# Masked first-token products, a deeper queue of raw weights and later bias reads in a two-layer hybrid attention block

## The chip, the cores and the metric

One core of a Trainium2 chip runs the whole program. The time is device microseconds of one execution, as the median of several. The engines are PE (TensorE, matmuls), DVE (VectorE), ACT (ScalarE), POOL (GpSimd) and SP (SyncE, which here only issues weight loads). Each works through its own instructions strictly in order and waits on semaphores for the others.

## What is computed

A sequence of 272 tokens (16 learned "meta" tokens, then 256 inputs) of width 1024 goes through two layers. Each layer has three kinds of attention on slices of one projection (A: eight heads that attend to the 64 keys an indexer scores highest; B: four differential heads; C: four retention heads), an output projection, and a feed-forward part with a squared ReLU. All is float32.

```python
h = concat([meta, x])                          # 272 x 1024
for l in range(2):
    u = rmsnorm(h, norm_mix[l])
    qa, ka, va, qi, ki, wi, qb, kb, vb, qc, kc, vc, gc = split(u @ w_in[l])
    a_out = sparse_indexer_attention(qa, ka, va, qi, ki, wi, bias_a, 64)
    b_out = rmsnorm(diff_attention(qb, kb, vb, bias_b, lam)) * (1 - lambda_init)
    ret = retention(rotary(qc), rotary(kc), vc)
    c_out = silu(gc) * rmsnorm(ret)
    h = h + concat([a_out, b_out, c_out]) @ w_out[l]
    h = h + square(relu(rmsnorm(h, norm_ff[l]) @ w_ff1[l])) @ w_ff2[l]
out = rmsnorm(h, final_norm)[16:]
```

Tokens are laid along the free axis in most tiles (128 features on the partitions, 272 tokens in a row). The first 16 tokens are handled apart from the two blocks of 128 tokens: their keys and values stand as small block-diagonal tiles, one block of 16 columns for each head that shares the 128 partitions, so that one matmul serves two or four heads.

## The kernel before

The weights are cut into 206 tiles of 128x1024 ("units"): in each layer 31 of the input projection, 8 of the output projection, 64 of the feed-forward part. A matmul in float32r loses low bits, so each unit is taken as two parts. ACT rounds the raw tile to `hi` (line 167), DVE or POOL makes `lo = raw - hi` (line 179; POOL for the units listed in `POOL_LO`), and PE runs three matmuls for each of eight slices, `hi` times the high part of the input, `hi` times its low part, `lo` times its high part (lines 186 to 188, 24 matmuls for a unit).

The program is one list written out by hand. The function `slot` (line 187 on) emits unit i: matmuls, and between them, at six places called evac, none, quarter, half, most and all, whatever was registered for this slot and place. In the middle of slot i stand `to_hi(i+3)`, `to_lo(i+2)` and `load(i+5)`. The table `PLACES` gives for each step of the attention numbers p; p // 6 is the slot in the layer, p % 6 the place in it. So "70" is slot 11, place "most". `AFTER` does the same relative to the unit whose product a step evacuates. What an engine does is thus in the order of these numbers, engine by engine, and a step that waits holds up what stands behind it on its engine.

Raw tiles come through `load` (line 147): one DMA of 512 KB on SP's queue into one of three buffers (`bufs=3`), so the load of unit i+5 waits until `lo` of unit i+2 has been made. The bias goes another way: `bias_write` puts a table into DRAM in 32 shifted copies (line 378, tile `scr`), and four calls of `bias_read` (line 383) fetch it, 32 partitions each and all 12 heads at once, into `nb`; `late_constants` (lines 345, 346) fetches rotary tables and decays. These are issued by ACT, on a queue of their own.

Steps that the change touches:

- `e_ki` (429, 430): the indexer's key is scaled into `kf`, then copied to `kh` by DVE.
- `e_v` (475 to 478): DVE scales a value unit out of PSUM into `vt` and copies two blocks of 64x16 into `vbdT`.
- `e_kbd` (507, 508): two DVE copies of 64x16 from the rotated key `kr`, which POOL has summed, into `kbdT`, four times two copies in all.
- `meta_softmax` (574 on), in the first layer alone, for the B heads (`b_soft`) and the A heads (`a_soft`): step one copies blocks from `kb` or `ka` into `kmB` or `kmA` on DVE (577, eight copies each); step two is two or four small matmuls, a bias, a minimum, a subtraction (592) and an exponential on ACT (593); step three sums and divides (601).
- `a_keys` (649) and `b_keys` (720): DVE copies the columns of the first tokens into `pm` and `wm`, 16 and 8 times.
- `b_pair`, `b_norm`, `b_keys`, `b_keys2`: scores of two B heads on PE, softmax on DVE and ACT, scaling on POOL (709), combination on DVE (714), transposes on PE.
- `a_bias` (617, 618), `a_pair`, `a_norm`, `a_keys`: the same for A heads, with mask plus bias on POOL.

Of the kernel before, what the change touches and what calls it, by code (L numbers as in the profile page):

```python
# [28 lines left out]
C_ID, C_ONES, C_COS, C_SIN, C_NEG, C_DEC, C_DECM, C_EXP = 0, 128, 256, 528, 800, 1072, 2608, 2880  # L29
C_ALL = 2896  # L30
P_MIX, P_FF, P_DN, P_RN = 0, 16, 32, 34
# [23 lines left out]
    "rot_tables": (99,),  # L55
    "e_kbd": (146, 157),
    "c_pair": (158, 163),
# [3 lines left out]
    "b_first": (91,),  # L61
    "b_soft": (76, 84, 86),
    "a_soft": (124, 130, 136),
    "a_pv": (175, 181, 187, 195),
    "factor": (11, 12, 17),
}

# [30 lines left out]
def block_kernel(ctx: ExitStack, tc: tile.TileContext, W, hin, cst, onehot, rbe, par, fin, dlam, out):  # L98
# [48 lines left out]
    def load(i, parts=1):  # L147
        if i >= DEPTH * N_UNITS or i in raws:
            return
        raw = wpool.tile([128, 8, 128], F, name="raw", bufs=3)  # L150
        n = 8 // parts
        for a in range(parts):
            nc.sync.dma_start(raw[:, a * n:a * n + n], W[i // N_UNITS, i % N_UNITS][:, a * n:a * n + n])
        raws[i] = raw
# [35 lines left out]
    def slot(i, ps, cols, xs, first=True, last=True, ks=tuple(range(8)), then=None):  # L190
        fire(i, "evac")
        fire(i, "none")
        if ps is None:
            ps = acc_bank()
        wt = split.pop(("hi", i)), split.pop(("lo", i))
        mm(ps[:, cols], wt, xs, ks[:2], first, False)
        fire(i, "quarter")
        mm(ps[:, cols], wt, xs, ks[2:4], False, False)
        if then is None:
            if i % N_UNITS != N_IN + 1:  # L200
                to_hi(i + 3)
# [12 lines left out]
        return ps, wt  # L214
# [13 lines left out]
    for _ in range(10):  # L228
        PE.matmul(idle[:, :128], z, z, start=True, stop=True)
    raws[0] = wpool.tile([128, 8, 128], F, name="raw", bufs=3)  # L230
    for a in range(0, 8, 2):
# [108 lines left out]
    to_hi(2)  # L340
    load(3)
    load(4)

    def late_constants():
        nc.scalar.dma_start(cs[:, C_COS:C_NEG], cst[:, C_COS:C_NEG])
        nc.scalar.dma_start(cs[:, C_DEC:C_EXP], cst[:, C_DEC:C_EXP])
# [33 lines left out]

    def bias_read(a):
        s = bcast["scr"]
        nc.scalar.dma_start(nb[32 * a:32 * a + 32],
                          bass.AP(tensor=s.tensor, offset=s.offset + 127 - 32 * a, ap=[[4799, 32], [400, 12], [1, T]]))

# [26 lines left out]
    def mixer(l):  # L412
# [6 lines left out]
        factor_to_rows(b, key, 0, False)  # L419

        def e_ki(ps):
            bc = bcast[key]
            f = ta("kf")
            k2 = ck([128, 2, T], R, "ki")
            kh, kl = k2[:, 0], k2[:, 1]
            V.tensor_tensor(f[64:128], ps[64:128, :T], bc[64:128], OP.mult)
            V.tensor_copy(kh[64:128], f[64:128])  # L430
# [27 lines left out]
        def e_mul(ps, name, m, n, n0, scale=None):  # L458
            bc = bcast[key]
            if name not in st:  # L460
                st[name] = ck([128, n, T], F, name)
            o = st[name][:, m, n0:]
            if scale is None:
                V.tensor_tensor(o, ps[:, n0:T], bc[:, n0:], OP.mult)  # L464
            else:
                V.scalar_tensor_tensor(o, ps[:, n0:T], scale, bc[:, n0:], OP.mult, OP.mult)

        def b_split(ps, name, m, n0, scale):
            if name not in st:
# [26 lines left out]
        def e_rot(ps, name, m, n0):  # L496
# [68 lines left out]

        def meta_softmax(name, plan, q, k, km, bias):

            tiles = km.shape[1]
            per = 8 // tiles
            rows = 128 // per  # L570
            x = {}

            def one():
                for i in range(tiles):
                    for a in range(per):
                        r = slice(rows * a, rows * a + rows)
                        V.tensor_copy(km[r, i, 16 * a:16 * a + 16], st[k][r, i, 0:16])  # L577

            def two():
# [23 lines left out]

            for p, f in zip(PLACES[plan], (one, two, three)):
                place(b, p, f)
# [105 lines left out]
        def b_keys(hd):  # L711
# [147 lines left out]

# [47 lines left out]
        def finish():  # L907
# [19 lines left out]
    def ffn_rows():  # L927
# [52 lines left out]
        def second(i, k):  # L980
# [138 lines left out]
def _constants(np):  # L1119
# [12 lines left out]
    for hd in range(4):  # L1132
# [78 lines left out]
```

## Time and profile before

| | us |
|---|---|
| median of 3 runs (740.35 to 743.11) | 741.5 |
| the profiled execution, device time | 742.43 |
| its span, first to last instruction | 740.6 |
| PE busy | 710.3 |
| DVE, ACT, POOL busy | 495.2, 374.5, 163.8 |

The span falls into the start (0 to 20 us), the first layer's attention ("first mixer", 20 to 146), output projection and feed-forward with the second layer's first units (146 to 403), the second layer's attention ("second mixer", 403 to 508), its output projection and feed-forward (508 to 730) and the last normalisation (730 to 741). Matmuls are pipelined, so a PE that is shown busy may still run at half its clock; the granted clock (PEclk) tells that.

### The profile page before, as it was taken

What the parts mean: (1) busy time and instruction counts of PE and PEld (TensorE: products, weight loads), DVE (VectorE), ACT (ScalarE), POOL (GpSimd) and SP (SyncE); (2) the same over time, 40 slices, a digit from 0 to 9 for tenths busy, and PEclk for the clock granted to TensorE, in tenths of its full rate; (3) what the DMA queues carried; (4) which work ended last, traced back from release to release, by engine and by line L of the source; (5) the groups of instructions that cost most, each with busy time, mean ns of one, the idle gap of its engine ahead of it and who ended that gap; (6) DMA issues with size and microseconds to landing.
All of it is one profiled execution on the core that took longest, in us unless ns stands there. A gap on an engine that the chain in (4) does not pass through costs nothing.

```text
span 740.6 us, 13376 instructions
## 1 busy us (share of the span) xinstructions
PE 710.3 (96%) x5248; PEld 666.3 (90%) x5248; DVE 495.2 (67%) x970; ACT 374.5 (51%) x695; POOL 163.8 (22%) x139
## 2 busy tenths in 40 slices
PE   8998899899999999999999998989999999999996
PEld 7987788789999999999999987978899998998995
DVE  6679869865877666464646897697486555555554
ACT  6425555435556555343435556553376445545543
POOL 3537544213200000000004758340140000000000
PEclk9999999899999999999999999998999999999998
DMA  7586323224545555646453533332356555555551
GB/s 233 140 223 219 97 105 108 77 76 141 191 155 195 171 171 172 190 156 195 156 187 114 176 121 117 108 107 86 114 170 221 178 186 196 188 177 206 186 171 57
DMA packets 34403, 115.53 MB, mean 156 GB/s; under 512 B 3971, under 2 KB 6308, under 8 KB 34340
## 3 DMA queue, kind: packets, MB, share of 16 engines
q1 hardware_dynamic: 31824, 111.00, 45.2%
q10 hardware_dynamic: 2516, 3.68, 2.4%
q8 instruction: 41, 0.67, 0.4%
q14 instruction: 22, 0.18, 0.1%
HBM read 113.00 MB, written 1.66 MB: 155 GB/s over the span
## 4 chain that ended last, share of the span: by engine, by line
PE 75%; DVE 15%; issue 3%; POOL 3%; DMA 3%; ACT 1%; SPq 0%; POOLq 0%; ACTq 0%; DVEq 0%
PE mm L186 19%; PE mm L188 19%; PE mm L187 18%; PE att L977 11%; DMA raw<-w 2%; DVE lo L179 2%; DVE acc L546 1%; DVE ry L503 1%; DVE m L544 1%; DVE wm L720 1%; POOL lo L179 1%; PE att L780 1%; DMA h<-hin 1%; DVE bp L555 1%; DVE kmB L577 1%
## 5 line engine op out<-in xcount | busy, mean ns | idle before, releaser
L167 ACT ACTIVATE hi<-raw 128x1024 fp32r<-128x1024 f32 x204 | 214.7, 1056 | 186.9 <-PE mm L187 133.0
L186 PE MATMUL mm<-uh,hi 128*128 128x272 f32 (+1 forms) x1008 | 298.6, 296 | 2.5 <-DVE ka L464 2.0
L188 PE MATMUL mm<-uh,lo 128*128 128x272 f32 (+1 forms) x1008 | 292.2, 290 | 3.5 <-POOL lo L179 2.7
L187 PE MATMUL mm<-ul,hi 128*128 128x272 f32 (+1 forms) x1008 | 291.1, 289 | 0.4
L179 DVE TENSOR_TENSOR lo<-raw,hi 128x1024 fp32r<-128x1024 f32 (+1 forms) x172 | 210.9, 1245 | 22.4 <-ACT hi L167 21.6
L186 PEld LDWEIGHTS mm<-uh,hi 128*128 128x128 f32 x1008 | 193.4, 192 | 10.1 <-issue 5.4
L188 PEld LDWEIGHTS mm<-uh,lo 128*128 128x128 f32 x1008 | 193.0, 191 | 5.0 <-POOL lo L179 3.6
L187 PEld LDWEIGHTS mm<-ul,hi 128*128 128x128 f32 x1008 | 193.6, 192 | 2.8 <-DVE ul L268 1.4
L179 POOL TENSOR_TENSOR lo<-raw,hi 128x1024 fp32r<-128x1024 f32 x36 | 87.8, 2447 | 75.7 <-ACT hi L167 63.3
L186 PE MATMUL mm<-sh,hi 128*128 128x272 f32 x256 | 74.2, 290 | 0.0
L188 PE MATMUL mm<-sh,lo 128*128 128x272 f32 x256 | 74.1, 289 | 0.0
L187 PE MATMUL mm<-sl,hi 128*128 128x272 f32 x256 | 73.7, 288 | 0.0
L276 POOL TENSOR_TENSOR sacc<-sacc,sq 128x272 f32<-128x272 f32 (+1 forms) x24 | 23.0, 957 | 206.4 <-ACT sq L274 206.1
L960 DVE TENSOR_TENSOR fr<-fr 128x256 f32<-128x256 f32 x32 | 13.6, 425 | 58.2 <-ACT fr L959 58.2
L187 PEld LDWEIGHTS mm<-sl,hi 128*128 128x128 f32 x256 | 48.3, 188 | 0.0
L186 PEld LDWEIGHTS mm<-sh,hi 128*128 128x128 f32 x256 | 48.2, 188 | 0.0
L188 PEld LDWEIGHTS mm<-sh,lo 128*128 128x128 f32 x256 | 48.2, 188 | 0.0
L1016 POOL TENSOR_TENSOR nr<-nv,cs 128x1 f32<-128x1 f32 x2 | 1.1, 561 | 178.9 <-DVE nv L1014 178.9
L977 PE MATMUL att<-hi,sh 128*128 128x512 f32 x128 | 40.2, 394 | 0.0
L977 PE MATMUL att<-hi,sl 128*128 128x512 f32 x128 | 40.2, 394 | 0.0
L186 PE MATMUL mm<-oh,hi 128*128 128x272 f32 (+1 forms) x128 | 36.9, 289 | 0.0
L187 PE MATMUL mm<-ol,hi 128*128 128x272 f32 (+1 forms) x128 | 36.6, 286 | 0.0
(237 smaller groups left out, 963.1 us busy)
## 6 DMA issues: line engine op xcount, KB each, us to landing
raw<-w SPq DMA_DIRECT2D x204, 512.0 KB, 3.6
nb<-scr ACTq DMA_DIRECT2D x4, 408.0 KB, 6.6
h<-hin SPq DMA_DIRECT2D x4, 272.0 KB, 4.7
raw<-w SPq DMA_DIRECT2D x4, 256.0 KB, 4.3
out_dram<-fo SPq DMA_DIRECT2D x4, 256.0 KB, 2.2
cs<-cst ACTq DMA_DIRECT2D x1, 904.0 KB, 5.6
scr<-row ACTq DMA_DIRECT2D x1, 600.0 KB
fg<-fin SPq DMA_DIRECT2D x1, 512.0 KB, 5.1
```

The costliest lines, as they stand in the source:

```text
L167: S.activation(hi[:, p], raw[:, p], AF.Copy)
L179: eng.tensor_tensor(lo[:, p], raw[:, p], hi[:, p].bitcast(F), OP.subtract)
L186: PE.matmul(ps, hi[:, k, :], xh, start=first and j == 0, stop=False)
L187: PE.matmul(ps, hi[:, k, :], xl, start=False, stop=False)
L188: PE.matmul(ps, lo[:, k, :], xh, start=False, stop=last and j == len(ks) - 1)
L276: eng.tensor_tensor(sacc[part][:, q0:], sacc[part][:, q0:], sq[:, q0:], OP.add)
L503: V.tensor_tensor(y[o:o + 32, n0:], ps[i:i + 32, n0:T], st["sinr"][i:i + 32, n0:], OP.mult)
L544: V.max(m, acc[:, sl])
L546: V.match_replace(acc[:, sl], m, acc[:, sl], MARK)
L555: V.tensor_tensor_reduce(t[:, T1], ps[:, T1], bias1, 1.0, 3.0e38, OP.add, OP.min, mn[:, 1:2])
L960: V.tensor_tensor(r[:, q0:], r[:, q0:], r[:, q0:], OP.mult)
L977: PE.matmul(acc[t, a], x, w[part][:, 512 * a:512 * a + 512], start=k == 0 and x is xh and part == 0, stop=k == 31 and part == 1)
```

## The change

Block-diagonal tiles are now made straight from PSUM by one multiplication with a mask. `block_factors` (slot 4) makes two factor tiles `bf` of 128x32 and 128x64, mask times the row factor of the first 16 tokens, and `blocks_of` multiplies a unit's first 16 columns, repeated two or four times, by such a factor. This takes the place of the copies into `vbdT`, `kmA` and `kmB`; `kbdT` becomes one POOL multiplication behind the POOL sum `kr`. The copies into `pm` and `wm` go from DVE to ACT, subtraction and division of `meta_softmax` from DVE to POOL, and `kh` is a product from PSUM and no copy.

Six buffers hold raw tiles, and slot i asks for unit i+8. Bias heads 8 to 11 (B) are read where all were read before; heads 0 to 7 (A) follow in slots 12 and 13; the constants follow in slots 14 and 20. A smaller DMA scratch makes room for the buffers.

```diff
-    "e_kbd": (146, 157),
-    "b_soft": (76, 84, 86),
-    "a_soft": (124, 130, 136),
+    "b_soft": (74, 84),
+    "a_soft": (124, 136),
+    "block_factors": (24,),
+NRAW = 6
-        raw = wpool.tile([128, 8, 128], F, name="raw", bufs=3)
+        raw = wpool.tile([128, 8, 128], F, name="raw", bufs=NRAW)
-            load(i + 5)
+            load(i + NRAW + 2)
-    at(13, "all", late_constants)
+    at(14, "half", late_constants, C_COS, C_NEG)
+    at(20, "half", late_constants, C_DEC, C_EXP)
-        for z in (vbdT, kbdT, kmA, kmB, smT[64:128]):
+        for z in (vbdT, smT[64:128]):
-        at(7 + a // 2, "all" if a % 2 else "half", bias_read, a)
+        at(7 + a // 2, "all" if a % 2 else "half", bias_read, a, 8, 4)
+        at(12 + a // 2, "all" if a % 2 else "half", bias_read, a, 0, 8)
+        def block_factors():
+            for n, mask in ((2, mask2), (4, mask4)):
+                f = small.tile([128, n, 16], F, name="bf%d" % n, bufs=1)
+                V.tensor_tensor(f, mask, bcast[key][:, None, 0:16].to_broadcast([128, n, 16]), OP.mult)
+                st["bf", n] = f
+        def blocks_of(dst, ps, n):
+            V.tensor_tensor(dst.rearrange("p (a c) -> p a c", a=n), ps[:, None, 0:16].to_broadcast([128, n, 16]),
+                            st["bf", n], OP.mult)
-            V.tensor_copy(kh[64:128], f[64:128])
+            V.tensor_tensor(kh[64:128], ps[64:128, :T], bc[64:128], OP.mult)
-            V.tensor_copy(vbdT[0:64, vs, c:c + 16], vt[0:64, 0:16])
-            V.tensor_copy(vbdT[64:128, vs, c + 16:c + 32], vt[64:128, 0:16])
+            blocks_of(vbdT[:, vs, c:c + 32], ps, 2)
-        def e_kbd(m):
-            V.tensor_copy(kbdT[0:64, m, 0:16], st["kr"][0:64, m, 0:16])
-            V.tensor_copy(kbdT[64:128, m, 16:32], st["kr"][64:128, m, 0:16])
+            if name == "kr":
+                G.tensor_tensor(kbdT[:, m].rearrange("p (a c) -> p a c", a=2),
+                                st[name][:, m, None, 0:16].to_broadcast([128, 2, 16]), mask2, OP.mult)
-                V.tensor_tensor(t, t, mn[:, :, None].to_broadcast([16, 8, 16]), OP.subtract)
+                G.tensor_tensor(t, t, mn[:, :, None].to_broadcast([16, 8, 16]), OP.subtract)
-                V.tensor_tensor(t, t, sm[:, :, None].to_broadcast([16, 8, 16]), OP.mult)
+                G.tensor_tensor(t, t, sm[:, :, None].to_broadcast([16, 8, 16]), OP.mult)
-            V.tensor_copy(st["pm"][:, :, hd, :], meta_cols(t))
+            S.activation(st["pm"][:, :, hd, :], meta_cols(t), AF.Copy)
-            V.tensor_copy(st["wm"][:, :, hd, :], meta_cols(w))
+            S.activation(st["wm"][:, :, hd, :], meta_cols(w), AF.Copy)
+    nc = _bacc.Bacc("TRN2", target_bir_lowering=False, num_devices=1, dynamic_dma_scratch_size=1024)
```

DVE in the first mixer, slots 12 and 13, behind the softmax of the first two B heads; `acc` is the indexer's score, `bsm` the B heads' sums. Before:

```order
L464 TENSOR_TENSOR ka<-mm,bc 128x272
L577 COPY kmB<-kb 32x16 x8
L707 TENSOR_SCALAR bsm<-bsm,lam 128x2
L714 SCALAR_TENSOR_TENSOR bp<-att,bsm,bp 128x272
L720 COPY wm<-bp 128x2x16
L586 TENSOR_TENSOR mt<-att,nb 16x128
L591 TENSOR_REDUCE mmn<-mt 16x8
L592 TENSOR_TENSOR mt<-mt,mmn 16x128
```

The same stretch now:

```order
L480 TENSOR_TENSOR ka<-mm,bc 128x272
L434 TENSOR_TENSOR kmA<-mm,bf_364 128x32
L597 TENSOR_TENSOR mt<-att,nb 16x128
L602 TENSOR_REDUCE mmn<-mt 16x8
L718 TENSOR_SCALAR bsm<-bsm,lam 128x2
L725 SCALAR_TENSOR_TENSOR bp<-att,bsm,bp 128x272
L610 TENSOR_REDUCE msm<-mt 16x8
```

The eight copies into `kmB` and the copies into `wm` are gone from DVE, the meta softmax of the B heads stands ahead of `bsm`, and its subtraction is no longer here (rows that did not move, the searches on `acc` among them, are left out).

POOL in the same slots; each `lo` is one unit's low part. Before:

```order
L179 TENSOR_TENSOR lo<-raw,hi 128x1024 x8
L709 TENSOR_SCALAR bp<-bp,bsm 128x144
L709 TENSOR_SCALAR bp<-bp,bsm 128x272
L179 TENSOR_TENSOR lo<-raw,hi 128x1024 x2
L617 TENSOR_TENSOR ap<-mask,nb 128x144
```

POOL now, from the seventh `lo` of that row on:

```order
L603 TENSOR_TENSOR mt<-mt,mmn 16x128
L180 TENSOR_TENSOR lo<-raw,hi 128x1024
L720 TENSOR_SCALAR bp<-bp,bsm 128x144
L720 TENSOR_SCALAR bp<-bp,bsm 128x272
L612 TENSOR_TENSOR mt<-mt,msm 16x128
L628 TENSOR_TENSOR ap<-mask,nb 128x144
```

A subtraction that waits for DVE (`mmn`) now stands ahead of the `lo` of unit 14, and a division that waits for DVE (`msm`) between the `lo` of units 15 and 16.

## Rows read from the trace of the kernel before

**Rows 1.** Page, part 1: busy us (share of span), instructions.

```profile
PE 710.3 (96%) x5248; PEld 666.3 (90%) x5248; DVE 495.2 (67%) x970; ACT 374.5 (51%) x695; POOL 163.8 (22%) x139
```

**Rows 2.** Stretches: length; busy PE, PEld, DVE, ACT, POOL; clock; DMA share; GB/s.

```profile
20.00:146.00 126.00, 113.09 (x825) 102.38 (x824) 102.92 (x293) 63.30 (x150) 61.47 (x51) 0.95 0.46 137
146.00:403.00 257.00, 257.00 (x2038) 252.62 (x2037) 158.91 (x224) 126.21 (x200) 24.33 (x19) 1.00 0.50 163
403.00:508.00 105.00, 97.10 (x756) 90.43 (x755) 85.31 (x243) 59.59 (x141) 56.26 (x44) 0.95 0.37 120
```

**Rows 3.** Waits of PE, 20 to 146 us: total us, times, longest.

```profile
PE att L760 <- DVE kbdT L508: 2.3, 1, 2.3
PE mm L188 <- POOL lo L179: 2.3, 2, 1.9
PE att L563 <- DVE bp L714: 2.2, 2, 2.0
PE mm L186 <- DVE ka L464: 2.0, 1, 2.0
PE att L627 <- DVE ol L831: 1.1, 1, 1.1
PE att L563 <- ACT ap L640: 0.9, 1, 0.9
PE att L533 <- DVE acc L538: 0.9, 1, 0.9
```

**Rows 4.** Waits of PE, 403 to 508 us.

```profile
PE att L760 <- DVE kbdT L508: 3.0, 1, 3.0
PE att L563 <- ACT ap L640: 2.1, 1, 2.1
PE att L487 <- DVE vt L475: 1.0, 1, 1.0
```

**Rows 5.** Stretches at half the clock.

```profile
60.50:63.90 3.40, 3.40 (x17) 3.40 (x16) 3.39 (x2) 3.33 (x14) 3.40 (x2) 0.50 0.58 205
...
139.00:145.80 6.80, 6.80 (x28) 6.15 (x29) 5.03 (x9) 1.82 (x5) 0.00 (x0) 0.50 0.14 55
...
500.80:507.60 6.80, 6.47 (x28) 5.87 (x28) 4.97 (x11) 1.91 (x5) 0.00 (x0) 0.50 0.23 77
```

**Rows 6.** Timeline of DVE: start us, us, instruction, count.

```profile
55.07 0.17 DVE L478 COPY vbdT<-vt 64x16 f32<-64x16 f32 x1
...
59.86 5.57 DVE L577 COPY kmB<-kb 32x16 f32<-32x16 f32 x8
...
135.09 2.29 DVE L508 COPY kbdT<-kr 64x16 f32<-64x16 f32 x1
...
424.59 2.35 DVE L478 COPY vbdT<-vt 64x16 f32<-64x16 f32 x1
```

**Rows 7.** Timeline of POOL.

```profile
89.15 1.76 POOL L618 TENSOR_TENSOR ap<-mask,nb 128x272 f32<-128x272 f32 x1
...
91.33 0.78 POOL L618 TENSOR_TENSOR ap<-mask,nb 128x272 f32<-128x272 f32 x1
...
135.01 2.35 POOL L179 TENSOR_TENSOR lo<-raw,hi 128x1024 fp32r<-128x1024 f32 x1
```

**Rows 8.** One ACT row; DMA queues from 44 to 54 us; page, part 6.

```profile
41.33 1.06 ACT L167 ACTIVATE hi<-raw 128x1024 fp32r<-128x1024 f32 x1 [5.05 <-DMA raw<-w]
...
q10 hardware_dynamic: 1600, 1.67, 85.6%
q1 hardware_dynamic: 52, 0.21, 9.8%
...
raw<-w SPq DMA_DIRECT2D x204, 512.0 KB, 3.6
```

**Rows 9.** Groups by form, whole span: busy us, mean ns of one, idle before.

```profile
L187 PE MATMUL mm<-ul,hi 128*128 128x272 f32 x640 | 187.8, 293 | 0.4
...
L475 DVE TENSOR_TENSOR vt<-mm,bc 128x272 f32<-128x272 f32 x16 | 7.0, 437 | 4.3 <-PE mm L188 4.2
...
L612 ACT ACTIVATE vm<-att 128x128 f32<-128x128 f32 x8 | 2.2, 274 | 0.0
```

More of the change, by code (lines that the diff above doesn't have):

```diff
@@ L29 @@
 C_ID, C_ONES, C_COS, C_SIN, C_NEG, C_DEC, C_DECM, C_EXP = 0, 128, 256, 528, 800, 1072, 2608, 2880
-C_ALL = 2896
+C_M2, C_M4, C_ALL = 2896, 2928, 2992
 P_MIX, P_FF, P_DN, P_RN = 0, 16, 32, 34
@@ L229, in block_kernel @@
         PE.matmul(idle[:, :128], z, z, start=True, stop=True)
-    raws[0] = wpool.tile([128, 8, 128], F, name="raw", bufs=3)
+    raws[0] = wpool.tile([128, 8, 128], F, name="raw", bufs=NRAW)
     for a in range(0, 8, 2):
@@ L249, in block_kernel @@
     nhalf = cs[:, C_EXP:C_EXP + 16]
+    mask2 = cs[:, C_M2:C_M4].rearrange("p (a c) -> p a c", a=2)
+    mask4 = cs[:, C_M4:].rearrange("p (a c) -> p a c", a=4)
     nb = const.tile([128, 12, T], F, name="nb")
@@ L340, in block_kernel, with late_constants @@
     to_hi(2)
[L341 to L346, printed above, removed]
-    at(13, "all", late_constants)
+    for i in range(3, NRAW + 2):
+        load(i)
+    def late_constants(a, z):
+        nc.scalar.dma_start(cs[:, a:z], cst[:, a:z])
+    at(14, "half", late_constants, C_COS, C_NEG)
+    at(20, "half", late_constants, C_DEC, C_EXP)
     def clear():
-        for z in (vbdT, kbdT, kmA, kmB, smT[64:128]):
+        for z in (vbdT, smT[64:128]):
             G.memset(z, 0.0)
@@ L379, in bias_write, with bias_read @@
         bcast["scr"] = scr[:]
-    def bias_read(a):
+    def bias_read(a, h0, n):
         s = bcast["scr"]
-        nc.scalar.dma_start(nb[32 * a:32 * a + 32],
-                          bass.AP(tensor=s.tensor, offset=s.offset + 127 - 32 * a, ap=[[4799, 32], [400, 12], [1, T]]))
+        nc.scalar.dma_start(nb[32 * a:32 * a + 32, h0:h0 + n],
+                            bass.AP(tensor=s.tensor, offset=s.offset + 127 - 32 * a + 400 * h0,
+                                    ap=[[4799, 32], [400, n], [1, T]]))
     def lambdas():
@@ L464, in e_mul @@
                 V.tensor_tensor(o, ps[:, n0:T], bc[:, n0:], OP.mult)
+                if first:
+                    blocks_of(kmA[:, m], ps, 2)
             else:
@@ L471, in b_split @@
             V.scalar_tensor_tensor(st[name][:, m, n0:], ps[:, n0:T], scale, bcast[key][:, n0:], OP.mult, OP.mult)
+            if first and name == "kb":
+                blocks_of(kmB[:, m], ps, 4)
         def e_v(ps, name, c0, vs):
@@ L564, in to_keys, with meta_softmax @@
             S.activation(dst, pt[:, :384], AF.Copy)
-        def meta_softmax(name, plan, q, k, km, bias):
+        def meta_softmax(name, plan, q, km, bias):
             tiles = km.shape[1]
             per = 8 // tiles
-            rows = 128 // per
             x = {}
[L573 to L577, printed above, removed]
             def two():
@@ L600, in three @@
                 V.reciprocal(sm, sm)
-                V.tensor_tensor(t, t, sm[:, :, None].to_broadcast([16, 8, 16]), OP.mult)
+                G.tensor_tensor(t, t, sm[:, :, None].to_broadcast([16, 8, 16]), OP.mult)
                 st[name] = t
-            for p, f in zip(PLACES[plan], (one, two, three)):
+            for p, f in zip(PLACES[plan], (two, three)):
                 place(b, p, f)
@@ L846, in mixer @@
         full = ("ki", "vb", "kb", "ka", "vc", "kr", "va")
-        for f in (e_wi2, i_mask, b_meta, rot_tables, c_meta, a_meta):
+        for f in (block_factors, e_wi2, i_mask, b_meta, rot_tables, c_meta, a_meta):
             place(b, PLACES[f.__name__][0], f)
         for f in (i_head, i_round, b_pair, b_norm, b_keys, b_keys2, a_bias, a_pair, a_norm, a_keys,
-                  r_pv, r_norm, r_scale, r_out, e_kbd, c_pair):
+                  r_pv, r_norm, r_scale, r_out, c_pair):
             for a, p in enumerate(PLACES[f.__name__]):
@@ L854, in mixer @@
         if first:
-            meta_softmax("bmeta", "b_soft", "qb", "kb", kmB,
+            meta_softmax("bmeta", "b_soft", "qb", kmB,
                          nb[0:16, 8:12, None, 144:160].to_broadcast([16, 4, 2, 16]))
             place(b, PLACES["b_first"][0], b_first)
-            meta_softmax("ameta", "a_soft", "qa", "ka", kmA, nb[0:16, 0:8, 144:160])
+            meta_softmax("ameta", "a_soft", "qa", kmA, nb[0:16, 0:8, 144:160])
         def after(i, f, *a):
@@ L912, in finish @@
             to_hi(b + N_IN + 5)
-            load(b + N_IN + 7)
+            load(b + N_IN + NRAW + 4)
         for m in range(8):
@@ L992, in second @@
             to_lo(i + 2)
-            load(i + 5)
+            load(i + NRAW + 2)
             fire(i, "half")
@@ L1137, in _constants @@
         c[16 * hd:16 * hd + 16, C_DECM:C_DECM + T] = g(q - np.arange(16)[:, None])
-    c[:, C_EXP:] = -0.5
+    c[:, C_EXP:C_M2] = -0.5
+    c[:, C_M2:C_M4] = p // 64 == np.arange(32)[None, :] // 16
+    c[:, C_M4:] = p // 32 == np.arange(64)[None, :] // 16
     dist = 271 - np.arange(400)
@@ L1202 @@
     arrays = _layout(np, inputs)
-    nc = _bacc.Bacc("TRN2", target_bir_lowering=False, num_devices=1)
+    nc = _bacc.Bacc("TRN2", target_bir_lowering=False, num_devices=1, dynamic_dma_scratch_size=1024)
     args = [nc.dram_tensor(n, v.shape, mybir.dt.from_np(v.dtype), kind="ExternalInput").ap()
```

## The prediction

> **What bounds the kernel now.** I read the page's shares of busy time first: PE is busy for 96% of the span, DVE for 67%, ACT for 51%, POOL for 22% [rows 1]. So PE is the bound, and only its idle time and its slow time can be won. The busy times by stretch then show where these lie [rows 2]. In the feed-forward stretch PE is busy for all of 257.00 us at a granted clock of 1.00, 2038 matmuls, one per 0.126 us; the change touches nothing there. The first mixer has 126.00 - 113.09 = 12.9 us of PE idle time and a mean clock of 0.95, the second mixer 105.00 - 97.10 = 7.9 us and the same clock. The 34 us that can be won at all are these 20.8 us, the slow clock and what goes with each wait (below).
>
> The waits of PE say who ends the idle time. First mixer: a `kbdT` copy 2.3, POOL's `lo` 2.3, `bp` 2.2, `ka` 2.0, `ol` 1.1, `ap` 0.9, `acc` 0.9, together 11.7 of 12.9 [rows 3]. Second: `kbdT` 3.0, `ap` 2.1, `vt` 1.0, together 6.1 of 7.9 [rows 4]. Most of them name DVE, which is far from full. The timeline shows why it is late [rows 6, 7]: a 64x16 copy into `vbdT` takes 0.17 us at 55.07 and 2.35 us at 424.59; the eight copies into `kmB` take 5.57 us where eight free ones would take 8 x 0.17 = 1.4; the `kbdT` copy at 135.09 takes 2.29 us and ends at 137.38, within 0.02 us of the 2.35-us `lo` that POOL began at 135.01. Such copies stand still while POOL works through a `lo`. DVE products that read PSUM don't: sixteen `vt` average 437 ns [rows 9].
>
> Last, the clock. Five stretches in the two mixers run at 0.50, that is 1.2 instead of 2.4 GHz; three have rows (3.40, 6.80 and 6.47 us of busy PE) [rows 5], the other two, at 84.4 and 459.9, are as long as the first. PE's busy time in them is 3 x 3.40 + 6.80 + 6.47 = 23.5 us, so 11.7 us are lost to the clock. Each begins within 2.5 us of the end of a PE wait of 1.9 us or more; behind waits of 1.1 us or less none begins. If the long waits go, the clock stays.
>
> **The change part by part**, against the profiled execution's 742.4 us.
>
> *Raw weights, minus 3.2.* A raw load lands in 3.6 us as a rule [rows 8], but the bias reads fill the DMA engines from 44 to 54 us: the bias queue had packets in flight for 85.6% of it and moved 1.67 MB, the weight queue only 0.21 MB [rows 8]. Before that, ACT stood 5.05 us for a raw tile until 41.33 [rows 8], so that the indexer's exponentials behind it, and with them `acc`, came late (0.9); later the late `hi` makes POOL's `lo` late (1.9, and 0.4 more) [rows 3]. Three more units of look-ahead at 24 x 0.126 = 3.0 us each are 9 us, and only a third of the bias is read there. That covers the hole, and I take 0.9 + 2.3 in full. The reads of heads 0 to 7, moved to slots 12 and 13, shut the weights out for some two thirds of 10 us there; eight units of look-ahead hide that.
>
> *DVE in the first mixer, minus 4.1.* `ka`, `bp` and `ap` (2.0 + 2.2 + 0.9) [rows 3] wait for a DVE that lost 5.57 - 1.4 = 4.2 us on `kmB` alone [rows 6]. The copies into `kmB`, `kmA`, `vbdT` are replaced by 22 masked products from PSUM and four for the factors, each smaller than a `vt` and so at most 0.44 us [rows 9], beside PE. `pm` and `wm` leave DVE too. I keep 1.0 of 5.1, because POOL gets more to do.
>
> *`ol`, minus 0.8*: of 1.1 [rows 3] behind the `kmA` copies I keep 0.3.
>
> *`kbdT`, minus 5.1.* The POOL product stands right behind the POOL sum it needs, so no `lo` can come between: 2.3 + 3.0 [rows 3, 4]. Its price lies between a free 128x272 POOL sum's 0.78 and a held one's 1.76 [rows 7] as upper ends, and its share of columns, an eighth of 0.78, as the lower. I keep 0.2.
>
> *Second mixer's `ap` and `vt`, minus 2.0*: of 3.1 [rows 4]. The `vbdT` copies and `pm` copies are gone from DVE, but `ap` goes through POOL's mask-plus-bias as well; 1.1 stays.
>
> *Smaller waits, minus 1.0*: the 1.2 + 1.8 us of idle time without rows; two thirds stay.
>
> *Restarts, minus 2.2.* A matmul is shown 0.293 us long [rows 9] though one follows the other in 0.126; the 0.167 us by which the last one overhangs is lost at each wait and counted as busy. Thirteen waits [rows 3, 4] give 2.2.
>
> *Clock, minus 10.0* of the 11.7; 1.7, one stretch of 3.4 us, stays.
>
> *New costs, plus 1.0.* ACT gets twelve small copies in each layer, each below the 0.274 us of a 128x128 one [rows 9], 3.3 us on an engine busy 63 of 126 us [rows 2]. The `wm` copies wait for DVE's `bp` ahead of `hi` of units 16 and on, and behind them stand PE's units; the three units between `hi` and its matmuls (9 us) cover that, and without cover it would be the 2.2 us that PE waits for `bp` now. On POOL the first layer's subtraction waits for DVE's `mmn` ahead of `lo` of unit 14, its division for `msm` ahead of `lo` of unit 16. Four such 16x128 operations cost at most 0.78 to 1.76 each [rows 7], 3 to 7 us, hidden unless `lo` has no slack; unit 14's has the least. Below, they could be worth a gain, as DVE is rid of them. Between -1 and +5 I take +1.0, nearest to the free 0.78-us row with one `lo` late. The smaller scratch and the late constants cost nothing while all DMAs go over the hardware queues that the rows show; both constants are read slots ahead of their use. `kh` was a copy and is a product: nothing.
>
> Sum: 3.2 + 4.1 + 0.8 + 5.1 + 2.0 + 1.0 + 2.2 + 10.0 - 1.0 = 27.4, so 715.0 for the profiled execution. It lay 0.9 above the median of 741.5, so 714.1, said as 714.
>
> **Rivals.** *POOL's chain becomes the next bound (722).* Against two-input DVE work POOL is itself held: the mask-plus-bias takes 1.76 us at 89.15 and 0.78 at 91.33 [rows 7]. The change gives POOL eight more small operations, four of which wait for DVE, in slots where it also makes nearly every `lo` at 2.35 us [rows 7] per 3.0 us of PE; its 61.47 us of 126 [rows 2] are crowded there. Then half of the terms `ka`/`bp`/`ap`, `ol` and second mixer returns, (4.1 + 0.8 + 2.0) / 2 = 3.5, and half of the clock's 10.0: 714 + 8.5 = 722. It decides once a `lo` is late by 1.9 us, the shortest wait behind which the clock fell. [...]
>
> *Everything comes back (707).* All idle time, restarts and clock: 742.4 - 20.8 - 2.2 - 11.7 = 707.7, less 0.9 = 706.8. For it: the waits all name a few causes. Against it: each wait hides a next one, and `ap` in the second mixer passes three engines.
>
> *DVE is not relieved (735).* If masked products were held like the copies, only the raw look-ahead would be won, 3.2, two restarts 0.3 and one or two clock stretches, 3: 742.4 - 6.5 - 0.9 = 735. The `vt` row speaks against it [rows 9].
>
> *Raw loads serialise (up to 803).* If the smaller scratch held each raw load until the one before had landed, a unit would come every 3.6 us [rows 8] and not every 3.03, as PE takes them: in the feed-forward stretches, 2038 / 24 = 85 units in 257.00 us [rows 2] and some 73 in the 222 us from 508 to 730, 0.57 x 158 = 90 us, 714 + 90 = 804, less with faster lone loads. It decides where a lone load takes longer than 3.03 us. Against it: the queues of the rows are hardware queues [rows 8], and POOL, which has no such work, issues none.
>
> **How the numbers follow.** Forecast 714: 0.56. POOL's chain, 722: 0.22. Everything back, 707: 0.14. DVE not relieved, 735: 0.05. Serialised loads: 0.03. The predicted time is the forecast's. The range reaches down to the third case with 2 us for what is modelled in matmul ends, 705, and up over the second with the upper bound of the new costs, 727; what lies outside is the last two cases and the edges of the others. Half a per cent (3.7 us) is about what a measurement of this kernel can tell from no change. Faster: the first three cases and nearly all of the fourth, 0.95; within it: 0.02, the rest of the fourth; slower: 0.03, the last.
>
> **What would show it.** Right: PE's idle time in the first mixer falls from 12.9 us to 4 to 5, with no wait for `kbdT`; at most one stretch at half the clock; no raw tile late for ACT from 41 to 60 us; masked products under 0.45 us whatever POOL does. Wrong: a wait for POOL's `lo` of units 14 to 18 or for `kbdT` at 1 us or more, with a half-clock stretch behind it (POOL's chain); masked products of 2 us (DVE not relieved); PE waiting for raw tiles in the feed-forward part (serialised loads).

## The result, and the profile after

| | before | changed |
|---|---|---|
| median, us | 741.4 (740.35 to 743.11) | 716.05 (715.14 to 716.76) |
| ratio to before | | 0.9655, 95% interval 0.9632 to 0.9678 |
| profiled execution: device time, span | 742.43, 740.6 | 715.46, 713.7 |

The changed kernel is 3.4% faster. The forecast was 714, the range 705 to 727. In the profiled executions the difference is 742.43 - 715.46 = 27.0 us; the sum of the prediction was 27.4.

Page, part 1, of the changed kernel, to be laid beside [rows 1]:

```profile
PE 696.9 (98%) x5248; PEld 657.1 (92%) x5248; DVE 464.6 (65%) x912; ACT 376.9 (53%) x719; POOL 168.2 (24%) x144
```

The number of matmuls is the same, 5248. PE is busy for 13.4 us less, and that is no work saved: some 10 of it is what the half clock cost. DVE has 58 instructions and 30.6 us less, ACT 24 instructions and POOL five more. ACT's 24 are the copies into `pm` and `wm`.

The stretches of the changed kernel that answer to those of [rows 2], in the same columns; the mixers are shorter by 16 and 11 us, and the feed-forward stretch between them (130 to 387) is still 257 us long:

```profile
20.00:130.00 110.00, 105.92 (x826) 97.26 (x826) 86.83 (x258) 64.47 (x159) 65.06 (x54) 0.98 0.53 157
387.00:481.00 94.00, 91.47 (x755) 86.30 (x754) 68.97 (x223) 60.16 (x149) 57.59 (x46) 1.00 0.40 134
```

PE's idle time in the first mixer is 110.00 - 105.92 = 4.1 us (12.9 before), in the second 94.00 - 91.47 = 2.5 (7.9 before). The mean clock rose from 0.95 to 0.98 and 1.00.

The waits of PE in the changed kernel, first mixer, then second (who is waited for: total us, times, longest), to be laid beside [rows 3, 4]:

```profile
PE att L581 <- ACT ap L651: 1.7, 1, 1.7
PE att L581 <- DVE bp L725: 0.8, 1, 0.8
PE att L506 <- DVE on L818: 0.5, 1, 0.5
PE att L506 <- DVE vt L495: 0.3, 1, 0.3
PE mm L189 <- POOL lo L180: 0.3, 1, 0.3
PE att L760 <- ACT vm L623: 0.2, 1, 0.2
PE mm L189 <- DVE lo L180: 0.2, 1, 0.2
...
PE att L581 <- ACT ap L651: 1.7, 1, 1.7
PE att L760 <- ACT vm L623: 0.8, 1, 0.8
```

No wait for `kbdT`, `ka`, `ol` or `acc` is left. What is left is above all the first A head's `ap`, 1.7 us in each layer. Of the five stretches at half the clock, one is left, from 84.1 to 87.5, right behind the first of these two waits:

```profile
84.10:87.40 3.30, 3.29 (x15) 3.05 (x14) 0.44 (x1) 2.90 (x8) 2.67 (x3) 0.50 0.25 52
```

The instructions that the change put in, grouped by form over the whole span (busy us, mean ns of one):

```profile
L434 DVE TENSOR_TENSOR vbdT<-mm,bf 128x32 f32<-128x32 f32 x16 | 2.9, 179 | 0.0
L434 DVE TENSOR_TENSOR kmA<-mm,bf 128x32 f32<-128x32 f32 x4 | 0.7, 174 | 0.0
L434 DVE TENSOR_TENSOR kmB<-mm,bf 128x64 f32<-128x64 f32 x2 | 0.4, 214 | 0.0
...
L660 ACT ACTIVATE pm<-ap 128x32 f32<-128x32 f32 x16 | 3.4, 215 | 0.0
L731 ACT ACTIVATE wm<-bp 128x32 f32<-128x32 f32 x8 | 1.8, 223 | 8.1 <-DVE bp L725 8.0
...
L525 POOL TENSOR_TENSOR kbdT<-kr,cs 128x32 f32<-128x32 f32 x4 | 4.5, 1115 | 0.3
```

All 22 masked products together take 4.0 us, none over 0.22. Three of them ran wholly beside a `lo` of POOL, in 0.22, 0.17 and 0.17 us; one with its `lo`:

```profile
65.28 0.17 DVE L434 TENSOR_TENSOR kmA<-mm,bf 128x32 f32<-128x32 f32 x1
...
64.07 2.40 POOL L180 TENSOR_TENSOR lo<-raw,hi 128x1024 fp32r<-128x1024 f32 x1
```

The ACT row of `wm` shows the new wait that the change brings: over the eight copies ACT stands 8.0 us in all for `bp`, ahead of `hi`, and no wait of PE names `hi`.

### The profile page after: what moved, and what is told of

It reads as the page before. It is cut to its first block, busy times and chain, and to the rows that moved or that the text cites. A ratio compares the mean times of both kernels' runs of the same rounds, so it can differ in the third digit from the quotient of the medians.

```text
span 713.7 us, 13335 instructions
## 1 busy us (share of the span) xinstructions
PE 696.9 (98%) x5248; PEld 657.1 (92%) x5248; DVE 464.6 (65%) x912; ACT 376.9 (53%) x719; POOL 168.2 (24%) x144
## 4 chain that ended last, share of the span: by engine, by line
PE 77%; DVE 12%; issue 3%; POOL 3%; ACT 2%; DMA 1%; SPq 0%; POOLq 0%; ACTq 0%; DVEq 0%
PE mm L187 20%; PE mm L189 19%; PE mm L188 19%; PE att L988 12%; DVE lo L180 2%; DVE ry L522 2%; DVE acc L564 1%; PE att L791 1%; DMA raw<-w 1%; DVE bp L573 1%; DVE bsm L718 1%; DVE m L562 1%; POOL lo L180 1%; PE att L785 1%; PE att L683 1%
## 5 line engine op out<-in xcount | busy, mean ns | idle before, releaser
L180 DVE TENSOR_TENSOR lo<-raw,hi 128x1024 fp32r<-128x1024 f32 (+1 forms) x172 | 215.7, 1273 | 23.2 <-ACT hi L168 21.4
L187 PEld LDWEIGHTS mm<-uh,hi 128*128 128x128 f32 x1008 | 191.0, 190 | 8.1 <-issue 4.5
L188 PEld LDWEIGHTS mm<-ul,hi 128*128 128x128 f32 x1008 | 191.0, 189 | 2.4 <-DVE ul L271 1.0
L189 PEld LDWEIGHTS mm<-uh,lo 128*128 128x128 f32 x1008 | 190.5, 189 | 2.0 <-DVE lo L180 1.5
L180 POOL TENSOR_TENSOR lo<-raw,hi 128x1024 fp32r<-128x1024 f32 x36 | 89.9, 2503 | 60.0 <-ACT hi L168 57.1
```

Source lines behind the costliest of these rows:

```text
L180: eng.tensor_tensor(lo[:, p], raw[:, p], hi[:, p].bitcast(F), OP.subtract)
L187: PE.matmul(ps, hi[:, k, :], xh, start=first and j == 0, stop=False)
L188: PE.matmul(ps, hi[:, k, :], xl, start=False, stop=False)
L189: PE.matmul(ps, lo[:, k, :], xh, start=False, stop=last and j == len(ks) - 1)
```

## The experiments

Times are medians; a ratio is against the kernel before on the same chip. All chips' times of before lay between 741.4 and 743.1.

| kernel | median, us | ratio, 95% interval |
|---|---|---|
| raws_alone (before + six buffers, smaller scratch) | 744.1 | 1.0025, 0.9999 to 1.0051 |
| raws_and_bias (raws_alone + bias in two parts) | 736.3 | 0.992, 0.9891 to 0.995 |
| kbd_alone (before + `kbdT` on POOL) | 732.3 | 0.9857, 0.9795 to 0.992 |
| lo28_on_dve (before, one `lo` moved) | 735.3 | 0.9904, 0.9876 to 0.9932 |
| raws_undone (changed, three buffers) | 718.0 | 0.9669, 0.962 to 0.9719 |
| bias_undone (changed, bias read at once) | 719.2 | 0.9689, 0.966 to 0.9717 |
| blocks_undone (changed, blocks copied) | 721.2 | 0.9716, 0.9668 to 0.9763 |
| pmwm_undone (changed, `pm`, `wm` on DVE) | 721.3 | 0.9716, 0.970 to 0.9733 |
| soft_undone (changed, meta softmax on DVE) | 715.4 | 0.9636, 0.9615 to 0.9657 |
| after_again (changed) | 714.8 | 0.9622, 0.9602 to 0.9642 |
| lo19_later (changed, one `lo` later) | 718.3 | 0.9668, 0.9592 to 0.9745 |
| lo19_norm (the same, two heads normalised earlier) | 719.1 | 0.9677, 0.9651 to 0.9703 |

**Six buffers alone.** The other requests follow in the same way, five tiles are asked for at the start where two were, and the smaller scratch is taken over.

```diff
-        raw = wpool.tile([128, 8, 128], F, name="raw", bufs=3)
+        raw = wpool.tile([128, 8, 128], F, name="raw", bufs=6)
-            load(i + 5)
+            load(i + 8)
```

> The kernel before with six raw buffers, the request eight ahead and the smaller scratch; bias reads, copies and products as before. Theory (a late raw tile makes `hi`, and so `acc` and POOL's `lo`, late): the waits for `acc` 0.9 and `lo` 2.3 go, two or three restarts 0.4, and the half-clock stretches at 60.5 and 84.4 with them, up to 3.4: 741.4 - 5.2 = 736, between 735 and 738. ACT stands for no raw tile from 35 to 60 us. Rival (these waits hang on the DVE queue, raw tiles are hidden): 741, with `acc` and `lo` waits as before. Serialised loads by the smaller scratch: 760 or more.

Nothing was won: 744.1, ratio 1.0025. The waits for `acc` and for POOL's `lo` did go, but a larger one came. Waits of PE in the first mixer:

```profile
PE mm L186 <- ACT att L557: 5.4, 1, 5.4
...
PE att L563 <- DVE bp L714: 2.2, 2, 2.0
PE mm L186 <- DVE ka L464: 2.1, 1, 2.1
```

DVE's timeline (the bracket is the idle time and what ended it) and the DMA issues from 40 to 64 us (KB each, median us from issue to landing) show what was waited for:

```profile
63.13 0.31 DVE L554 CUSTOM_DVE_ANT_0 bp<-att,nb 128x144 f32<-128x144 f32 x1 [7.97 <-DMA nb<-scr]
...
raw<-w SPq DMA_DIRECT2D x6, 512.0 KB, 10.0
nb<-scr ACTq DMA_DIRECT2D x4, 408.0 KB, 17.6
```

The bias reads, which landed in 6.6 us in the kernel before, now take 17.6: with more weights asked for, the weight queue moves 4.17 MB from 40 to 64 us where it moved 3.40, and the bias comes late for the softmax of the first two B heads. Neither theory had this. The weights hardly wait for the bias any more (ACT stands once for a raw tile, 1.1 us); the bias waits for the weights.

**Six buffers, and the bias in two parts.** To the edit above comes the change's `bias_read` with its head range, `(a, 8, 4)` in slots 7 and 8 and `(a, 0, 8)` in slots 12 and 13.

> The kernel before with six raw buffers, the request eight ahead, the smaller scratch, and the bias read in two parts (heads 8 to 11 where all were read, heads 0 to 7 in slots 12 and 13). Theory after raws_alone (deeper weight requests took the DMA engines from the bias, whose four reads landed 17.6 us after issue, so that PE stood 5.44 us behind the first B softmax): with a third of the bias there, that wait is gone and the waits for `acc` and `lo` too: 735 to 738. Rival (the weight queue still starves the bias): 740 to 744 with DVE standing for `nb` by 3 us or more.

736.3, as the theory had it. PE's waits in the first mixer, the largest:

```profile
PE att L762 <- DVE kbdT L510: 2.3, 1, 2.3
PE att L565 <- DVE bp L716: 2.2, 2, 2.0
PE mm L186 <- DVE ka L466: 2.0, 1, 2.0
```

`acc`, the 1.9-us `lo` and the wait for the bias are all gone, and what is left is above all the DVE queue. So the deeper queue wins something only with the bias in two parts. The other half by itself, the bias in two parts with three buffers, was not run on the kernel before, so how much of this gain it would bring alone is not shown.

**The bias read at once, in the changed kernel.**

```diff
-        at(7 + a // 2, "all" if a % 2 else "half", bias_read, a, 8, 4)
-        at(12 + a // 2, "all" if a % 2 else "half", bias_read, a, 0, 8)
+        at(7 + a // 2, "all" if a % 2 else "half", bias_read, a, 0, 12)
```

> The changed kernel with all twelve heads of the bias read in slots 7 and 8. Theory: the reads land late as in raws_alone, DVE and then PE stand 4 to 6 us in slot 13 and the clock falls for up to 6.8 us: 720 to 725. Rival (the bias split brings nothing, the look-ahead everything): 716.

719.2, a little under the range. Its interval overlaps the first one of the changed kernel (0.9632 to 0.9678) and not that of after_again (0.9602 to 0.9642), so a price is likely and its size open. PE's waits:

```profile
PE mm L189 <- POOL lo L180: 2.6, 1, 2.6
PE mm L187 <- DVE bmn L572: 2.5, 1, 2.5
```

DVE stood 7.24 us for `nb` in this run, and PE 2.5 behind the softmax that it delayed; the `lo` of 2.6 came behind that.

**Three buffers, in the changed kernel.** `NRAW = 3`.

> The changed kernel with three raw buffers and the request five ahead. If the look-ahead does the work: the holes of ACT return where the bias is written and read, 3 to 5 us, 719 to 721. Rival (reading only a third of the bias early is enough by itself): 716 to 717.

718.0, but its interval (0.962 to 0.9719) holds the changed kernel's ratio, so the price of this part by itself stays open between none and some 5 us. The trace speaks for a price: ACT stands 2.60 us for a raw tile until 44.95 (0.74 in the changed kernel) and PE 2.0 us for `vt` at 52.8 (0.3). A stretch at half the clock begins there, but the one at 84 is missing in turn.

**`kbdT` alone.** The POOL product of the change put into the kernel before, `e_kbd` taken out.

> The kernel before with nothing but `kbdT` made by the POOL product. Theory: both `kbdT` waits go (2.3 + 3.0, less 0.2), two restarts 0.3 and the two clock stretches behind them (half of 6.80 and of 6.47, 6.6): 741.4 - 12.0 = 729, between 728 and 731, no half clock at 139 and 500. Rival (the next thing is late right behind, or the clock falls anyway): 734 to 738.

732.3, 9 us of the 12 expected. Both waits for `kbdT` are gone, and so are the half-clock stretches of the end of each mixer. What is missing are smaller things: ACT's `vm` comes up behind the second `kbdT` (0.8), PE waits 2.1 for `ap` in the first mixer (0.9 before), and half-clock stretches came behind that and in the start (96.4 to 99.7, 7.7 to 11.0), against one that stayed away in the second mixer. Early in the first mixer one wait took another's place, where the edit touches nothing. DVE and POOL make a `lo` each there:

```profile
44.27 5.70 POOL L178 TENSOR_TENSOR lo<-raw,hi 128x1024 fp32r<-128x1024 f32 x2 [6.16 <-ACT hi L166]
44.59 3.15 DVE L178 TENSOR_TENSOR lo<-raw,hi 128x1024 fp32r<-128x1024 f32 x1
```

In the kernel before, DVE's began 0.36 us ahead of POOL's, which began at 45.04:

```profile
44.68 1.21 DVE L179 TENSOR_TENSOR lo<-raw,hi 128x1024 fp32r<-128x1024 f32 x1
```

Here POOL came first by 0.32 us, and DVE's took 3.15 instead of 1.21; PE waited 2.3 us for it, with a stretch of 3.4 us at half the clock behind. In return the wait of 1.9 us for a POOL `lo` and the stretch at 60.5, which the kernel before had, are gone. Which of the two came first was decided by a raw tile's landing: in the kernel before, ACT's `hi` ahead of POOL's `lo` stood 0.62 us for it.

**One `lo` moved.**

```diff
-POOL_LO = (5, 6, 7, 8, 10, 11, 12, 13, 14, 15, 16, 17, 18, 20, 24, 28, 34, 36)
+POOL_LO = (5, 6, 7, 8, 10, 11, 12, 13, 14, 15, 16, 17, 18, 20, 24, 34, 36)
```

> The kernel before with one entry taken from the list of units whose `lo` POOL makes (28, the one that ran from 135.01 and from 497.71 while DVE copied `kbdT`); DVE makes it, behind the copies. Theory (a DVE copy stands while POOL works through a `lo`): the last copy into `kbdT` takes 0.17 us instead of 2.29, both waits of 2.3 and 3.0 go and the half clock behind them: 729 to 733, about what kbd_alone gave. Rival (the copy is slow by itself, or waits for its source): a copy of 2 us, 741.

This is the cleanest test of the cause. The copy is the same instruction in the same place of DVE's queue; only POOL no longer works beside it:

```profile
135.64 0.69 DVE L507 COPY kbdT<-kr 64x16 f32<-64x16 f32 x1
136.34 0.17 DVE L508 COPY kbdT<-kr 64x16 f32<-64x16 f32 x1
```

0.17 us instead of 2.29 [rows 6]. That a DVE copy from SBUF to SBUF stands while POOL works through a `lo` is shown. The copy ahead of it still takes 0.69 and ends at 136.33, and POOL makes the sum `qr` beside it until 136.30: what holds a copy need not be a `lo`. The time, 735.3, lies above the range: 0.9 us of wait for `kbdT` stayed in the second mixer, with a half-clock stretch from 496.5 to 499.8 behind it, and the early collision of kbd_alone came here too.

**Blocks copied again, in the changed kernel.** The calls of `blocks_of` taken out, DVE copies into `vbdT`, `kmA`, `kmB` put back, the last two at the places 124 and 74, directly ahead of the matmuls that read them.

> The changed kernel with the blocks of `vbdT`, `kmA` and `kmB` copied by DVE from SBUF again, 16 + 8 + 8 + 16 copies more; all else as changed. Theory (copies held by POOL's `lo` made DVE late): copies of 2 us and more appear, waits for `bp`, `ka` or `vt` return, 3 to 6 us and up to one clock stretch of 1.7: 719 to 724. Rival (what relieved DVE were `pm`, `wm` and the meta softmax): 716 to 717.5 with no copy over 0.5 us in a place that PE waits for.

721.2, in the range, but half the reason is another. Groups of the copies (mean ns of one), then PE at the matmuls that read `kmB`:

```profile
L493 DVE COPY vbdT<-vt 64x16 f32<-64x16 f32 x16 | 5.1, 321 | 0.6
L494 DVE COPY vbdT<-vt 64x16 f32<-64x16 f32 x16 | 5.0, 310 | 0.2
L592 DVE COPY kmA<-ka 64x16 f32<-64x16 f32 x8 | 1.3, 167 | 0.1
L592 DVE COPY kmB<-kb 32x16 f32<-32x16 f32 x8 | 1.3, 164 | 0.1
...
59.51 0.37 PE L597 MATMUL att<-kmB,qb 128*16 128x64 f32 x2 [3.13 <-ACT bp L573]
```

Some `vbdT` copies were held (a mean of 0.31 to 0.32 where a free one takes 0.17), those into `kmA` and `kmB` not at all (0.16 to 0.17). PE waits 3.13 us for `kmB` and 1.5 for `kmA`, with 6.8 us at half the clock behind the first, because the copies stand behind the softmax of `b_pair` on DVE; the trace puts the first wait down to ACT, but the eight copies began at 58.68 and the matmul at 59.51, when the first four were done. So for these two tiles the product is worth something because it is made where its unit is evacuated. My placing of the copies right ahead of the reader made that worse than it was before, so this run doesn't price the contention.

**`pm` and `wm` on DVE again, in the changed kernel.**

```diff
-            S.activation(st["wm"][:, :, hd, :], meta_cols(w), AF.Copy)
+            V.tensor_copy(st["wm"][:, :, hd, :], meta_cols(w))
```

(and the same for `pm`)

> The changed kernel with the 24 copies into `pm` and `wm` on DVE again. Before, the `wm` copies took 1.72 us in the middle (0.30 at best) since POOL worked through a `lo` beside them. Theory: 8 x 1.4 us of DVE time come back around `bp` and the mask, so that PE's wait for `bp` grows from 0.8 to about 2 and the clock falls once: 718 to 721. Rival (they lie beside PE work): 715.5 to 717.

721.3, 6.5 us above the changed kernel on the same chip, just over the range of the theory. One copy and the `lo` beside it:

```profile
74.83 1.82 DVE L731 COPY wm<-bp 128x32 f32<-128x32 f32 x1
...
74.23 2.39 POOL L180 TENSOR_TENSOR lo<-raw,hi 128x1024 fp32r<-128x1024 f32 x1
```

The copy ends at 76.65, the `lo` at 76.62. PE's wait for `bp` is 2.0 (0.8 in the changed kernel), for `ap` 2.0 and 2.1 (1.7 each). Most of the copies' time is contention: the 24 of them take 18.5 us on DVE, where at the shortest of each kind (0.31 and 0.16) they would take 5. This is the largest single part of the relief of DVE that a run could price.

**Meta softmax on DVE again, in the changed kernel.** `G.tensor_tensor` to `V.tensor_tensor` at the subtraction and the division.

> The changed kernel with the subtraction and the division of the first layer's meta softmax on DVE again. Theory (they lay off the path, and on POOL they hold up `lo` 14 and 16 by 0.4 us each): no difference, 715.5 to 717. Rival one (POOL is the next bound in slots 12 to 18): 713 to 715, as `lo` comes earlier. Rival two (on DVE each is held by a `lo` and `bp` is late): 718 or more.

715.4 against 714.8 of the changed kernel on the same chip, intervals overlapping: no difference that can be told. PE's wait for `bp` in the first mixer is 1.5 instead of 0.8; it cost nothing behind it. Nothing was won either, so nothing speaks for POOL as the bound in slots 12 to 18.

**The changed kernel again.**

> The changed kernel once more, on the same chip as the others of this call: 716, 715 to 717.

714.8. In the profiled execution the clock fell behind both waits for `ap`.

**Trying to remove the last waits.** In the changed kernel a DVE `lo` (unit 19) holds POOL's first mask-plus-bias for 1.48 us. First it was put later:

```diff
-LATE_LO = (1, 13, 15, 18, 30, 35, 36, 37, 38)
+LATE_LO = (1, 13, 15, 17, 18, 30, 35, 36, 37, 38)
```

> The changed kernel with the `lo` of unit 19, which DVE makes, put behind the softmax of the first two A heads (17 added to LATE_LO). In the changed kernel this 2.64-us `lo` at 77.15 and at 432.67 holds POOL's first mask-plus-bias (1.48 instead of 0.49), and PE then stands 1.70 us for the first A head twice, the only stretch at half the clock behind one of them. Theory: each wait shrinks by 1.0 and the clock stays: 716 - 2.0 - 1.7 = 712, between 711 and 714. Rival (the wait's chain runs through ACT, or unit 19 becomes late): 715 to 718.

Its four times spread from 713.5 to 724.8, so the time tells nothing. The trace tells more: the mask-plus-bias takes 0.49 us and the exponentials come 1.1 us earlier, as expected, but the two waits grew from 1.7 to 2.05 and 2.02, because the reciprocal that `ap` needs now stood behind the `lo` on DVE. In this execution the clock stayed at 1.00 behind both. So the reciprocal was put ahead of the `lo`:

```diff
-    "a_norm": (109, 110, 119, 127, 137, 144, 155, 156),
+    "a_norm": (105, 105, 119, 127, 137, 144, 155, 156),
```

> The changed kernel with the `lo` of unit 19 behind the softmax of the first two A heads, as in lo19_later, and the normalisation of these two heads (a_norm) moved from slot 18 to behind their softmax, so that DVE's reciprocal stands ahead of that `lo` and ACT's scaling ahead of the last B transposes' copy. In lo19_later the exponentials came 1.1 us earlier but the reciprocal waited behind the `lo` (81.40 to 83.26). Theory: the two waits of 1.7 us for the first A head fall to 0.3 to 0.8 each and no clock stretch is left in the mixers: 2 x 1.1 + 1.7 = 4 below after_again, 711 to 713. Rival (unit 19 becomes late, or another wait stands behind): no difference, 715 to 717.

719.1 against 714.8 on the same chip, the intervals apart: slower, which neither the theory nor the rival (no difference) had, though the rival's reason, unit 19 late, came. PE's waits around it, DVE's `lo`, and POOL beside it:

```profile
PE mm L189 <- DVE lo L180: 2.5, 1, 2.5
PE att L581 <- ACT ap L651: 0.4, 1, 0.4
...
82.47 4.51 DVE L180 TENSOR_TENSOR lo<-raw,hi 128x1024 fp32r<-128x1024 f32 x1
...
82.37 2.37 POOL L180 TENSOR_TENSOR lo<-raw,hi 128x1024 fp32r<-128x1024 f32 x1
84.70 0.49 POOL L628 TENSOR_TENSOR ap<-mask,nb 128x144 f32<-128x144 f32 x1
85.15 0.75 POOL L629 TENSOR_TENSOR ap<-mask,nb 128x272 f32<-128x272 f32 x1
```

The waits for `ap` fell from 1.7 to 0.4, as meant. But the `lo` now begins 0.10 us behind POOL's own and is held until POOL has no instruction left at 85.9: 4.51 us for what takes 1.2 in the clear. PE waits 2.5 and 1.4 us for unit 19 instead. A version that beats the changed kernel was not found.

## Why the prediction was right, point by point

**Where time can be won.** Right. In the stretch of 257 us PE runs 2038 matmuls without a break before and after, and all 27 us came from the mixers: 20.8 us of PE idle time fell to 6.6.

**Raw weights, 3.2 forecast.** Of the waits for `acc` (0.9) and `lo` (2.3), 0.3 is left with POOL and 0.2 with DVE: 2.7 came. The size was nearly right and the reason half right. The prediction gave the gain to the look-ahead and named the smaller first read of the bias as a help; raws_alone shows that the look-ahead by itself wins nothing in the kernel before, since it moves the shortage from the weights to the bias (17.6 us to landing). The two together give it (736.3). What the smaller first read would give alone is open; in the changed kernel, with three buffers, it leaves 0.3 us of waiting for POOL's `lo`. The sign "no raw tile late for ACT from 41 to 60 us" was missed by one wait of 0.74 us at 44.64.

**DVE in the first mixer, 4.1 forecast.** `ka` went (2.0), `bp` fell from 2.2 to 0.8, but `ap` rose from 0.9 to 1.7: 2.6 came. This term was mis-sized, and the sign of `ap` was wrong. The prediction kept 1.0 for POOL's added work; what holds `ap` in the changed kernel is in part POOL's mask-plus-bias held by a DVE `lo` (1.48 instead of 0.49; lo19_later), and that POOL work is not new. The operations that were moved to POOL are not it: with the meta softmax back on DVE (soft_undone) the wait is 1.7 as well, and the `kbdT` products come later.

**`kmB` as the cause.** The prediction read 4.2 us lost on `kmB` copies, from one execution, and gave the waits for `ka` and `bp` to them. In raws_alone and raws_and_bias, where they are the same copies in the same place, they took 1.43 us and were not held, and PE still waited 2.0 to 2.1 us for `ka` and 2.0 for `bp`. In the kernel before, what stands ahead of that `ka` on DVE was itself held by POOL:

```profile
68.99 4.68 POOL L179 TENSOR_TENSOR lo<-raw,hi 128x1024 fp32r<-128x1024 f32 x2
...
69.77 1.63 DVE L720 COPY wm<-bp 128x32 f32<-128x32 f32 x1
...
71.93 1.88 DVE L592 TENSOR_TENSOR mt<-mt,mmn 16x128 f32<-16x128 f32 x1
73.74 0.42 DVE L464 TENSOR_TENSOR ka<-mm,bc 128x272 f32<-128x272 f32 x1
```

A `wm` copy takes 0.29 us where it is free, and the division of the meta softmax, as large as this subtraction, 0.28. Both have left DVE. Neither pmwm_undone nor soft_undone brings the wait for `ka` back, and the order of these steps changed too, so which of them removed it is not shown. What the runs price is `wm` and `pm` (pmwm_undone: 6.5 us), of which the prediction said only that they leave DVE. The mechanism was right, the copies on which it bites most were others.

**`ol`, 0.8 forecast.** Its wait went whole; a new one for `on`, 0.5, came. 0.6.

**`kbdT`, 5.1 forecast.** Both waits went; ACT's `vm` came up behind them, 0.2 and 0.8: 4.3. The product takes 1.115 us, inside the bounds, though not by its columns: the 128x272 sum ahead of it takes 0.77. PE doesn't wait for it. kbd_alone won 9 us by itself (6 to 15 by its interval), clock and restarts included, by the medians the largest part that one edit gave.

**Second mixer, 2.0 forecast; smaller waits, 1.0.** `ap` 1.7 stays of 3.1: 1.4 came. Of the idle time without rows, 3.0, the wait for `vt` in the first mixer, 0.3, and 0.1 of rounding are left: the waits shown (4.0 + 2.5) make up the 6.6 us of idle time but for that. 2.6 came where 1.0 was forecast, and that this made up for the DVE term (2.6 of 4.1) is luck.

**Restarts and clock, 2.2 and 10.0 forecast.** One stretch of 3.4 us stayed of five, as said: 11.7 - 1.7 = 10.0. To hit it so closely was luck as well: two stretches stayed in the profiled execution of after_again, and none in that of lo19_later, whose waits for `ap` were longer. PE's busy time in the mixers fell by 113.09 - 105.92 + 97.10 - 91.47 = 12.8; less the clock's 10.0, 2.8 are left. The prediction counted thirteen restarts where its rows have twelve (2.0 us), and some waits stayed, so 2.8 is more than restarts of its size explain; nothing measures them by themselves. With 14.2 us of idle time gone the three make 27.0, which is the whole difference.

**New costs, 1.0 forecast.** POOL's `lo` is late once, 0.3 us, counted above with the raw weights. ACT's wait for `bp` ahead of `hi` is covered, as argued.

**The rivals.** POOL's chain (722): no; POOL's row in [rows 2] grew from 61.47 to 65.06 us in a stretch 16 us shorter, and the `lo` in question is 0.3 late. What the rival had of the truth is the mutual holding of DVE and POOL, and it is what stopped lo19_norm. The Trainium skill, "SBUF — State Buffer", section "Who interferes with whom", says that a DVE instruction in one of its 2-port modes, which a copy can enter, contends with GpSimd (POOL), the first to issue blocking the other for the whole instruction, and that outside these modes one with at most one SBUF input does not contend. lo28_on_dve (a copy, 2.29 against 0.17) and the masked products (0.22 at most, one input from PSUM) agree with it. Everything back (707): no, because the two waits for `ap` stayed. DVE not relieved (735): no, by the masked products. Serialised loads: no; a raw tile lands in 3.6 us as before.

## What to carry to other kernels

Before giving a queue a deeper look-ahead, ask what else uses the DMA engines at that time: here the deeper weight queue only moved the shortage to the bias until the bias was read in two parts. Small copies on DVE beside long POOL work are better made on ACT, or as a product straight from PSUM at evacuation, since here it was the neighbour and not the copy's size that set its price (0.17 or 2.29 us for the same copy). And a wait that looks removable by order alone should be checked for whom the moved instruction then runs beside.

## What the runs showed of the hardware that was not expected

Whether the engine that waits gets its turn between two instructions of the other varies. In the first layer of lo19_norm DVE's `lo` was held over three POOL instructions in a row, 4.51 us instead of 1.2. In the second layer of the same execution the `lo` in the same place also began 0.10 us behind POOL's. It ended 1.1 us behind that one's end, so it got its turn there, and POOL's next instruction took 1.47 instead of 0.49:

```profile
439.53 3.35 DVE L180 TENSOR_TENSOR lo<-raw,hi 128x1024 fp32r<-128x1024 f32 x1
...
439.43 2.37 POOL L180 TENSOR_TENSOR lo<-raw,hi 128x1024 fp32r<-128x1024 f32 x1
441.76 1.47 POOL L628 TENSOR_TENSOR ap<-mask,nb 128x144 f32<-128x144 f32 x1
```

What decides between the two is open. And a lead of 0.3 us decides who is held (kbd_alone: 3.15 us against 1.21 in the kernel before), so when a raw tile lands can decide which engine loses time.

The clock was less regular than the prediction read from one trace (shortest wait with a fall behind it: 1.9 us). In that trace itself no fall follows PE's wait of 1.99 us for `ka`, which ended at 74.31. In the changed kernel it fell behind a wait of 1.70 that ended at 83.94 and not behind one of 1.68 that ended at 439.47; in after_again it fell behind both, 1.72 and 1.71. In kbd_alone a wait of 2.09 us, which ended at 455.7, had no fall behind it, nor had those of 2.05 and 2.02 in lo19_later; in lo28_on_dve a fall came behind waits of 0.86 and 0.33, 2.3 us after the end of the first. In PE's timeline of the changed kernel, then of after_again:

```profile
439.47 0.85 PE L581 MATMUL att<-cs,ap 128*128 128x128 f32 x3 [1.68 <-ACT ap L651]
...
438.69 0.85 PE L581 MATMUL att<-cs,ap 128*128 128x128 f32 x3 [1.71 <-ACT ap L651]
```

What decides between them stays open.
